# Expert gates: one-hot rows from one broadcast comparison on VectorE, multiplied by the gates on GpSimd

## Chip, cores and metric

One core of one Trainium2 chip runs the whole program in one launch. The metric is device time in microseconds (us); three runs of the kernel before gave 3524.37 us as the median (3522.42 to 3524.39).

## What is computed

Two transformer blocks over 256 tokens of width 2048. The change lies in the last sublayer, a mixture of 16384 single-neuron experts. Each expert is a pair (first key, second key) out of 128 x 128; each of 8 heads chooses 16 of them per token, so 128 slots per token. Cut to what matters:

```python
q = (hb @ w_query).reshape(PEER_BLOCK, PEER_HEADS, 2, D_KEY // 2)
s = jnp.einsum('thpc,hpnc->thpn', q, sub_keys).astype(jnp.float32)
top_s, top_i = lax.top_k(s, PEER_TOPK)
...
best_s, best_j = lax.top_k(cand_s, PEER_TOPK)
idx = jnp.take_along_axis(cand_i, best_j, axis=-1)
g = jax.nn.softmax(best_s, axis=-1)
u_sel = jnp.take(u, idx, axis=0)
a = jax.nn.gelu(jnp.einsum('thkd,td->thk', u_sel, hb), approximate=False)
v_sel = jnp.take(v, idx, axis=0)
return jnp.einsum('thk,thkd->td', (g * a).astype(hb.dtype), v_sel)
```

## The kernel before

**The weight products.** Every large product takes its weights as 128x128 blocks, eight to a DMA of 512 KB. `half` (L285) turns each load into two tiles of four blocks in two parts: ScalarE copies the high part `whi` (through `acp`, L275), VectorE subtracts it from the block for the low part `wlo` (through `vtt`, L260). Four tiles of each part are kept. `linear` makes three TensorE products per block (`mm`, L254): weight high part by activation high part, by activation low part, and weight low part by activation high part.

**The expert stage** (`experts_in`, L1569) does not gather experts. It computes gelu(h . u) of all 16384, in 128 columns of 16 blocks: column c is second key c, with the first keys on the partitions. `expert` (L1605) empties a column: VectorE multiplies the accumulator by the tokens' scale into a tile `et` (two buffers), ScalarE applies the gelu (L272), and for tokens whose gates are known GpSimd multiplies it with the gates that stand in `A` (`gtt`, L257). After the last column, `experts_out` (L1745) multiplies `A` with the second table of weights.

**The gates** (`gates`, L1626) are worked out beside these products, two tokens at a time, 128 pairs of tokens. For a token, slots lie on the partitions. `TI` and `TJ` hold for each slot and token the first and the second key, `TG` the gate in two parts. A tensor_scalar on VectorE compares a row of 0 to 127 (`iota`, in the tile named `ones`) with the slot's first key: `Pt`, a one-hot row per slot (`ts`, L267). Two more tensor_scalars compare with the second key and multiply by one part of the gate: `Qt`, two one-hot rows scaled (L269). TensorE multiplies `Pt` by `Qt` into `pG`: the sum over slots, [first key, part, second key]. `add` (L1634) adds the two parts (ScalarE copies one out, VectorE adds the other: the tile `G`, one buffer), and GpSimd then writes four pieces of `A` for these two tokens: a product (L257) for columns that are done, a copy (L1645) for columns to come.

**The order.** `drive` (L326) goes through the weight blocks and after every sixth takes one step of a stream; here the stream is the choice of keys for tokens 0 to 127 (`choose`), that for tokens 128 to 255, and `gates`. `gates` has two steps per pair: the one-hot rows; then the product `pG` and the `add` of the pair before. With `pace=(1,)` a step's instructions may not issue before the last `wlo` emitted so far. The framework's planner, from its own costs, sets the order on each engine; the engines then work in that order and wait by semaphores. The loads of weights carry high priority.

The lines that make the rows:

```python
Pt = sp.tile([128, n, 128], F32R, name="Pt", tag="Pt", bufs=2)
Qt = [sp.tile([128, 2, 128], F32R, name="Qt", tag="Qt", bufs=3) for _ in range(n)]
for t in range(n):
    o = slice(t0 + t, t0 + t + 1)
    self.ts(Pt[:, t], iota, self.TI[:, o], None, OP.is_equal)
    a, b = divmod(t0 + t, 16)
    for i in range(2):
        self.ts(Qt[t][:, i], iota, self.TJ[:, o], tg[i][:, a, b:b + 1], OP.is_equal, OP.mult)
```

Of the kernel before, what the change touches and what calls it, by code (L numbers as in the profile page):

```python
# [8 lines left out]
F32 = mybir.dt.float32  # L9
# [19 lines left out]
# ---------------------------------------------------------------- host layout  # L29


def _const_arrays():
    """Constants that follow from the shapes alone: name -> [128, width]."""
# [73 lines left out]
# w_in columns in the order in which they are worked on, as (first column, count) pieces of 128-column tiles  # L107
# [25 lines left out]
def _blocks(w, order="cols", group=None):  # L133
    """[K, N] -> [n, 128, 8, 128]: 128x128 blocks in the order in which they are used, eight to a load."""
    k, n = w.shape
    b = w.reshape(k // 128, 128, n // 128, 128)
    if group is None:
        b = b.transpose(2, 0, 1, 3).reshape(-1, 128, 128)
    else:
        kt = k // 128  # L140
        b = b.reshape(kt // group, group, 128, n // 128, 128).transpose(0, 3, 1, 2, 4).reshape(-1, 128, 128)
    return np.ascontiguousarray(b.reshape(-1, 8, 128, 128).transpose(0, 2, 1, 3))


def _pcol(v):
    """[128 * n] -> [128, n]"""
    return np.ascontiguousarray(np.asarray(v).reshape(-1, 128).T)
# [30 lines left out]
def _tT(x):  # L178
    """[T, 2048] -> [128, 16, T]"""
    x = np.asarray(x)  # L180
    return np.ascontiguousarray(x.reshape(x.shape[0], KT, 128).transpose(2, 1, 0))
# [40 lines left out]
# ---------------------------------------------------------------- kernel  # L222
# [4 lines left out]
# weight blocks between the stages of the streams beside them: block 1 (three streams), block 2, the experts  # L227
EVERY1, EVERY2, EVERY3 = (6, 6, 7), 8, 6
QB = 4  # weight blocks in a tile of parts
RAW, PARTS = 4, 4  # tiles of weights as they come; of their high and of their low parts  # L230
# [13 lines left out]
class Kernel:  # L244
# [7 lines left out]
    # ---- small helpers  # L252
# [31 lines left out]
    # ---- weight stream: 128x128 blocks as two float32r parts whose sum is the block  # L284
# [20 lines left out]
    def linear(self, w, h0, ncol, nkt, xh, xl, n, evac, t0=0, c0=0, more=()):  # L305
        """out[col] = sum_kt w[kt, col].T @ (xh + xl)[kt]; n tokens from t0; evac(col, psum)."""
        blk = h0 * 8
        cur = None
        for c in range(c0, c0 + ncol):
            p = self.ps("plin") if c in more else self.plin.tile([128, 512], F32, name="plin", tag="plin")  # L310
            nn = n(c) if callable(n) else n
            tt = t0(c) if callable(t0) else t0
            xs = slice(tt, tt + nn)
            for kt in range(nkt):
                if blk % 8 == 0 or cur is None:
                    cur = self.ahead.pop(0) if self.ahead else self.half(w[blk // 8])
                b = blk % 8
                hi, lo = (self.block(x, b) for x in cur)
                self.mm(p[:, :nn], hi, xh[:, kt, xs], kt == 0, False)
                self.mm(p[:, :nn], hi, xl[:, kt, xs], False, False)  # L320
                self.mm(p[:, :nn], lo, xh[:, kt, xs], False, kt == nkt - 1)
                blk += 1
                yield
            evac(c, p[:, :nn])

    def drive(self, dense, streams, every, pace=(), flush=True):  # L326
        """Emits the weight products with the stages of the other streams between them."""
# [26 lines left out]
    def split(self, hi, lo, src, scale=None):  # L354
        """src (* scale) as hi + lo, float32r each."""
        if scale is None:
            self.acp(hi, src)
            self.vtt(lo, src, hi.bitcast(F32), OP.subtract)
        else:
            self.acp(hi, src, scale=scale)  # L360
            self.stt(lo, src, scale, hi.bitcast(F32), OP.mult, OP.subtract)

    def rsqrt(self, y, x, scale=None, eps=None, floor=None):
        """y = 1 / sqrt(x * scale + eps) for a few columns (x in PSUM or SBUF): Newton from an exponent guess."""
# [15 lines left out]
    def colsum(self, srcs, n):  # L380
        """sum over partitions (and over the tiles srcs) by token -> psum [tokens, block]."""
# [7 lines left out]
    def bcast(self, dst, r, n, o=0):  # L389
        """r [token, block] -> dst [128, n]: the token's value in every partition."""  # L390
# [9 lines left out]
    # ---- whole program  # L400
# [23 lines left out]
    # ---- block 1: RWKV group and sparse attention group  # L424
    def load_norm(self, src, gain, xh, xl, dst, eps, acc, w, tiles):
        """x^T * gain as two parts, and dst = the tokens' 1 / rms in every partition; the first weights come between."""
# [18 lines left out]
    def squares(self, t, acc, first, pool=False):  # L445
        """acc (+)= the squares of a tile [feature, 4, token], in two parts; the tile is overwritten"""
# [17 lines left out]
    def block1(self, c0):  # L464
# [33 lines left out]
        def loads():  # L498
            """the constants, behind the weights that are wanted sooner"""
# [74 lines left out]
        def hold(what):  # L574
            """the recurrent group's stages up to the one that frees a tile"""
# [38 lines left out]
    def inv_sqrt(self, r, x, t):  # L614
        """r = x ** -0.5: an exponential, and a step of Newton's; t is scratch"""
# [6 lines left out]
    def rwkv_group(self, g, AR, K, V, fr):  # L622
# [14 lines left out]
        # decay: exp of minus the running sum, inside chunks of 64 tokens  # L637
# [9 lines left out]
        # unit keys  # L647
# [4 lines left out]
        # decay: exp of minus the running sum, inside chunks of 64 tokens  # L652
# [6 lines left out]
        # token-major copies: partition (chunk parity, token)  # L659
# [14 lines left out]
        # k' = k (1 + (a - 1) k_a)  # L674
# [10 lines left out]
        # scaled factors: A = -kk W_{t-1}, R = r W_t, B = kk a / W_t, K = k' / W_t  # L685
# [24 lines left out]
        # Gram matrices, transposed: [s, (t of A | t of R)]  # L710
# [19 lines left out]
        # F = T^T, T = (I - N)^-1: 32-row diagonal blocks by doubling the block size, then the block below them  # L730
# [25 lines left out]
        # U = T (A S' + A_k V) = P S' + Q  # L756
# [79 lines left out]
        # from chunk to chunk: S' = W_C (M S + R), M = I + B'^T P, R = B'^T Q + K'^T V  # L836
# [47 lines left out]
        # y^T [v, t]  # L884
# [23 lines left out]
        # group norm per head, gate  # L908
# [24 lines left out]
    # ---- sparse attention group  # L933
# [12 lines left out]
    def tables(self):  # L946
        """cosines and sines of the rotary angles, by feature and token"""
# [45 lines left out]
    def rope(self, dst, rot, d):  # L993
        """dst = rope(dst / rms) in place."""
# [58 lines left out]
    def dsa_topk(self):  # L1053
        """mb = 0 where a key is among the 64 best causal ones of its query, else -1e30."""
# [50 lines left out]
    # ---- the rest of block 1  # L1105
    def norm_tile(self, k, src, gain, xh, xl, acc, pool):
        """one feature tile of the next product's input, and its squares"""
# [56 lines left out]
    def cross(self, cp, cxh, cxl, rc):  # L1164
# [57 lines left out]
        # the first columns' products with the heads that are done, between the stages of the last head  # L1222
# [29 lines left out]
    def mlp(self, up):  # L1252
# [43 lines left out]
        # x1 = h g_f r1; block 2 normalises x1: r12 = r1 * rsqrt(r1^2 mean((h g_f)^2) + eps)  # L1296
# [13 lines left out]
    def meta_tokens(self):  # L1310
        """their part of block 2's normalised input"""
# [19 lines left out]
    # ---- block 2: stick-breaking and forgetting attention  # L1331
    def block2(self):
# [33 lines left out]
        def forget(p):  # L1366
            """B16, X16: rows from which a product of 16 gives the sums of log f between two tokens"""
# [14 lines left out]
        def values(t):  # L1382
            """[feature, token] -> [token, block, feature]"""
# [8 lines left out]
        def stick(hd, q_, k_, v_):  # L1392
# [16 lines left out]
            # sums of softplus over the visible keys from s on  # L1409
# [19 lines left out]
        def fox(hd, q_, k_, v_):  # L1429
            # q and k normalised over the head's features  # L1430
# [59 lines left out]
        def merge(acc, src, gain, o, name):  # L1490
            """heads normalised over 1024 features (and gated), as parts of the next product's input"""
# [60 lines left out]
        # token-major copy of the residual, kept in DRAM until the end  # L1552
# [15 lines left out]
    # ---- experts  # L1568
    def experts_in(self):  # L1569
        """gelu(h . u) of every expert, feature rows of the first key on partitions; meanwhile the choice of experts."""  # L1570
# [7 lines left out]
        self.TI, self.TJ = (sp.tile([128, S], F32, name=n) for n in ("TI", "TJ"))  # L1578
        # the gates' two parts, in the columns of the meta tokens, which are free here
# [25 lines left out]
        def expert(c, p):  # L1605
# [4 lines left out]
            t = sp.tile([128, S], F32, name="et", tag="et", bufs=2)  # L1610
# [15 lines left out]
    def gates(self, slot):  # L1626
        """A[first key, second key, token] *= summed gates of the chosen pairs (kept there where A is still to come)"""
# [21 lines left out]
        tg = [x.bitcast(F32) for x in self.TG]  # L1649
        for t0 in range(0, S, n):  # L1650
            yield
            Pt = sp.tile([128, n, 128], F32R, name="Pt", tag="Pt", bufs=2)
            Qt = [sp.tile([128, 2, 128], F32R, name="Qt", tag="Qt", bufs=3) for _ in range(n)]
            for t in range(n):
                o = slice(t0 + t, t0 + t + 1)
                self.ts(Pt[:, t], iota, self.TI[:, o], None, OP.is_equal)
                a, b = divmod(t0 + t, 16)
                for i in range(2):
                    self.ts(Qt[t][:, i], iota, self.TJ[:, o], tg[i][:, a, b:b + 1], OP.is_equal, OP.mult)
            yield  # L1660
            p = self.ps("pG").rearrange("p (t i j) -> p t i j", t=n, i=2)
            for t in range(n):
                self.mm(p[:, t], Pt[:, t], Qt[t])
# [6 lines left out]
    def choose(self, tb, sc, buf, big):  # L1670
        """The 16 best pairs of keys per head, and their softmax: TI, TJ, TG [slot = (head, rank), token]."""
# [68 lines left out]
        for i, t in enumerate((self.TI, self.TJ)):  # L1740
            self.acp(t[:, ts], p[:, 128 * i:128 * i + 128])
# [51 lines left out]
```

## Time and profile before

| what | value |
|---|---|
| median of three runs | 3524.37 us |
| span of the profiled execution | 3527.4 us |
| PE (TensorE matmul) busy | 3471.3 us, 98% |
| DVE (VectorE) busy | 2502.3 us, 71% |
| ACT (ScalarE) busy | 1814.6 us, 51% |
| POOL (GpSimd) busy | 671.6 us, 19% |
| moved by DMA | 602.39 MB, 171 GB/s |
| expert columns, first to last emptied | 2053.3 to 2823.4 us |
| gates, first to last one-hot row | 2237.7 to 2816.0 us |

The profile is of one further execution. The page gives its span, from the first to the last instruction, and no other time for it; the span is 3.0 us (0.09%) over the median of the timed runs. Matmuls overlap, so "PE 98%" says that TensorE always had one in flight, not that it ran at its peak; how many matmuls start in a stretch says how fast it went. A row's idle time is that of its engine, and what ended it is inferred from semaphores.

### The profile page before, as it was taken

The numbers are of one execution on the slowest core, as the hardware profiler recorded it, in microseconds if no ns is written. First come the engines' busy times: TensorE is split into PE (matmuls) and PEld (weight loads), VectorE is DVE, ScalarE is ACT, GpSimd is POOL, SyncE is SP. The second block draws the span as 40 slices with busy tenths as digits, with TensorE's granted clock in tenths as the row PEclk, the third lists the DMA queues.
The fourth block names the chain that finished last, engine by engine and source line by source line (L and its number), as shares of the span: only waits on it lengthen the run. The fifth ranks groups of instructions, "written<-read, shape, count | busy, mean of one in ns | idle before, by whom it ended". The sixth has DMA issues, their size and how long they took to land.

```text
span 3527.4 us, 74174 instructions
## 1 busy us (share of the span) xinstructions
PE 3471.3 (98%) x28638; PEld 3277.4 (93%) x28638; DVE 2502.3 (71%) x5118; ACT 1814.6 (51%) x3416; POOL 671.6 (19%) x1142
## 2 busy tenths in 40 slices
PE   8999999999999999999999999999999999999999
PEld 7899889899999999999999999999999988888887
DVE  7678767765656568556567589999999955555555
ACT  5444555554545455444445444555555555555554
POOL 2222213310101015200012001344445500000000
PEclk9999999999999999999999999999999999999999
DMA  5334536466666666544446655555565566666665
GB/s 195 112 118 129 163 112 189 134 186 184 186 182 186 184 186 183 154 145 143 121 130 186 200 179 163 166 177 178 176 178 177 176 210 193 195 192 195 193 193 183
DMA packets 165779, 602.39 MB, mean 171 GB/s; under 512 B 18384, under 2 KB 19088, under 8 KB 165040
## 3 DMA queue, kind: packets, MB, share of 16 engines
q1 hardware_dynamic: 165424, 597.65, 56.3%
q8 instruction: 224, 3.67, 0.4%
q14 instruction: 131, 1.07, 0.1%
HBM read 593.38 MB, written 4.19 MB: 169 GB/s over the span
## 4 chain that ended last, share of the span: by engine, by line
PE 94%; DVE 4%; issue 1%; DMA 1%; POOL 0%; ACT 0%; DVEq 0%; SPq 0%; ACTq 0%; POOLq 0%
PE plin L254 66%; PE o L254 20%; DVE wlo L260 2%; PE pG L254 1%; PE po L254 1%; PE pfz L254 1%; PE pw L254 0%; PE pz L254 0%; PE pbc L254 0%; PE pix L254 0%; PE pcs L254 0%; DVE xl L263 0%; PE pt L750 0%; PE px L750 0%; PE py L254 0%
## 5 line engine op out<-in xcount | busy, mean ns | idle before, releaser
L260 DVE TENSOR_TENSOR wlo<-raw,whi 128x512 fp32r<-128x512 f32 x2208 | 1610.7, 733 | 809.3 <-ACT whi L275 761.2
L275 ACT ACTIVATE whi<-raw 128x512 fp32r<-128x512 f32 x2208 | 1389.2, 631 | 1333.2 <-PE plin L254 936.6
L254 PE MATMUL plin<-ph,wlo 128*128 128x256 f32 (+1 forms) x4560 | 1290.6, 284 | 11.0 <-DVE wlo L260 11.0
L254 PE MATMUL plin<-ph,whi 128*128 128x256 f32 (+1 forms) x4560 | 1287.9, 283 | 1.6 <-DVE ut L260 0.7
L254 PE MATMUL plin<-pl,whi 128*128 128x256 f32 (+1 forms) x4560 | 1288.7, 283 | 0.0
L254 PEld LDWEIGHTS plin<-ph,wlo 128*128 128x128 f32 x4560 | 863.4, 190 | 15.8 <-DVE wlo L260 13.5
L254 PEld LDWEIGHTS plin<-ph,whi 128*128 128x128 f32 x4560 | 864.1, 190 | 3.0 <-issue 1.6
L254 PEld LDWEIGHTS plin<-pl,whi 128*128 128x128 f32 x4560 | 861.2, 189 | 1.6 <-issue 1.1
L254 PE MATMUL o<-wlo,wh 128*128 128x512 f32 x1024 | 399.1, 390 | 0.0
L254 PE MATMUL o<-whi,wl 128*128 128x512 f32 x1024 | 397.2, 389 | 0.0
L254 PE MATMUL plin<-xh,whi 128*128 128x256 f32 x1136 | 330.6, 292 | 8.7 <-ACT whi L275 8.2
L254 PE MATMUL plin<-xh,wlo 128*128 128x256 f32 x1136 | 329.8, 291 | 3.4 <-DVE wlo L260 3.2
L254 PE MATMUL plin<-xl,whi 128*128 128x256 f32 x1136 | 329.5, 290 | 1.7 <-DVE xl L263 1.7
L254 PE MATMUL o<-whi,wh 128*128 128x512 f32 x1024 | 316.6, 390 | 1.9 <-ACT wh L275 1.9
L254 PE MATMUL plin<-uh,wlo 128*128 128x256 f32 x1024 | 289.7, 283 | 0.0
L254 PE MATMUL plin<-ul,whi 128*128 128x256 f32 x1024 | 289.7, 283 | 0.0
L254 PE MATMUL plin<-uh,whi 128*128 128x256 f32 x1024 | 289.6, 283 | 0.0
L254 PEld LDWEIGHTS plin<-xh,whi 128*128 128x128 f32 x1136 | 222.0, 196 | 13.6 <-ACT whi L275 9.4
L254 PEld LDWEIGHTS o<-whi,wh 128*128 128x128 f32 x1024 | 192.8, 188 | 42.2 <-ACT wh L275 2.1
L254 PEld LDWEIGHTS plin<-xh,wlo 128*128 128x128 f32 x1136 | 221.7, 195 | 10.2 <-DVE wlo L260 5.2
L254 PEld LDWEIGHTS o<-wlo,wh 128*128 128x128 f32 x1024 | 192.8, 188 | 40.2
L254 PEld LDWEIGHTS o<-whi,wl 128*128 128x128 f32 x1024 | 192.1, 188 | 39.9
(571 smaller groups left out, 3866.1 us busy)
## 6 DMA issues: line engine op xcount, KB each, us to landing
raw<-in_pu_dram SPq DMA_DIRECT2D x256, 512.0 KB, 3.7
raw<-in_pv_dram SPq DMA_DIRECT2D x256, 512.0 KB, 4.3
raw<-in_w_in_dram SPq DMA_DIRECT2D x208, 512.0 KB, 3.6
raw<-in_w_up_dram SPq DMA_DIRECT2D x128, 512.0 KB, 4.3
raw<-in_w_down_dram SPq DMA_DIRECT2D x128, 512.0 KB, 4.2
raw<-in_w_mix_dram SPq DMA_DIRECT2D x32, 512.0 KB, 3.7
raw<-in_w_out_dram SPq DMA_DIRECT2D x32, 512.0 KB, 3.7
raw<-in_w_pq_dram SPq DMA_DIRECT2D x32, 512.0 KB, 3.7
```

The source lines that it names most:

```text
L254: self.nc.tensor.matmul(out, l, r, start=start, stop=stop)
L260: return self.nc.vector.tensor_tensor(out, a, b, op=op)
L275: return self.nc.scalar.activation(out, a, AF.Copy, **kw)
```

## The change

For a pair of tokens, the one-hot rows of both tokens and of both keys are made by one tensor_tensor comparison on VectorE, whose two operands are repeated: `iota` over tokens and keys, and the key indices (now interleaved in one tile `TIJ`) over the 128 positions. GpSimd then multiplies the second key's rows of both tokens by the high part of the gates and, in another instruction, by the low part. The scaled rows `Q` have one buffer, the one-hot rows `E` two; `et` has one buffer where it had two. Texts of comments are dropped too. The core of the diff:

```diff
@@ experts_in
-        self.TI, self.TJ = (sp.tile([128, S], F32, name=n) for n in ("TI", "TJ"))
+        self.TIJ = sp.tile([128, S, 2], F32, name="TIJ")
...
-            t = sp.tile([128, S], F32, name="et", tag="et", bufs=2)
+            t = sp.tile([128, S], F32, name="et", tag="et", bufs=1)
@@ gates
+        sh = [128, n, 2, 128]
         for t0 in range(0, S, n):
             yield
-            Pt = sp.tile([128, n, 128], F32R, name="Pt", tag="Pt", bufs=2)
-            Qt = [sp.tile([128, 2, 128], F32R, name="Qt", tag="Qt", bufs=3) for _ in range(n)]
-            for t in range(n):
-                o = slice(t0 + t, t0 + t + 1)
-                self.ts(Pt[:, t], iota, self.TI[:, o], None, OP.is_equal)
-                a, b = divmod(t0 + t, 16)
-                for i in range(2):
-                    self.ts(Qt[t][:, i], iota, self.TJ[:, o], tg[i][:, a, b:b + 1], OP.is_equal, OP.mult)
+
+            E = sp.tile(sh, F32R, name="E", tag="E", bufs=2)
+            self.vtt(E, iota[:, None, None, :].to_broadcast(sh), self.TIJ[:, t0:t0 + n, :, None].to_broadcast(sh),
+                     OP.is_equal)
+            Q = sp.tile(sh, F32R, name="Q", tag="Q", bufs=1)
+            a, b = divmod(t0, 16)
+            for i in range(2):
+                self.gtt(Q[:, :, i], E[:, :, 1].bitcast(F32), tg[i][:, a, b:b + n, None].to_broadcast([128, n, 128]),
+                         OP.mult)
             yield
             p = self.ps("pG").rearrange("p (t i j) -> p t i j", t=n, i=2)
             for t in range(n):
-                self.mm(p[:, t], Pt[:, t], Qt[t])
+                self.mm(p[:, t], E[:, t, 0], Q[:, t])
@@ choose
-        for i, t in enumerate((self.TI, self.TJ)):
-            self.acp(t[:, ts], p[:, 128 * i:128 * i + 128])
+        for i in range(2):
+            self.acp(self.TIJ[:, ts, i], p[:, 128 * i:128 * i + 128])
```

## Rows read from the trace of the kernel before

**Rows 1.** The page: busy time of each engine, and the 40 slices.
```profile
PE 3471.3 (98%) x28638; PEld 3277.4 (93%) x28638; DVE 2502.3 (71%) x5118; ACT 1814.6 (51%) x3416; POOL 671.6 (19%) x1142
...
PE   8999999999999999999999999999999999999999
...
DVE  7678767765656568556567589999999955555555
...
POOL 2222213310101015200012001344445500000000
```

**Rows 2.** The page: the chain that ended last, by engine.
```profile
PE 94%; DVE 4%; issue 1%; DMA 1%; POOL 0%; ACT 0%; DVEq 0%; SPq 0%; ACTq 0%; POOLq 0%
```

**Rows 3.** Windows of 100 us: length, then PE, PEld, DVE, ACT, POOL; clock; DMA.
```profile
2200.00:2300.00 100.00, 93.95 (x757) 92.56 (x756) 96.22 (x222) 50.69 (x102) 33.73 (x61) 0.97 0.54 165
2300.00:2400.00 100.00, 100.00 (x851) 100.00 (x850) 92.25 (x241) 58.59 (x125) 43.56 (x135) 1.00 0.58 178
...
2500.00:2600.00 100.00, 100.00 (x851) 100.00 (x850) 95.42 (x242) 58.20 (x123) 49.00 (x127) 1.00 0.61 179
...
2700.00:2800.00 100.00, 100.00 (x850) 100.00 (x850) 100.00 (x240) 55.71 (x121) 56.18 (x130) 1.00 0.60 176
```

**Rows 4.** Windows of 20 us around the start and the end of the gates.
```profile
2240.00:2260.00 20.00, 16.24 (x117) 15.46 (x118) 20.00 (x34) 8.77 (x19) 6.75 (x6) 0.91 0.36 112
...
2800.00:2820.00 20.00, 20.00 (x172) 20.00 (x171) 18.65 (x42) 10.07 (x25) 12.15 (x25) 1.00 0.58 177
```

**Rows 5.** Waits of PE from 2050 to 2900 us: total, times, longest.
```profile
PE plin L254 <- DVE wlo L260: 8.7, 9, 2.4
PE pG L254 <- DVE Qt L269: 2.9, 2, 2.6
PE o L254 <- ACT wh L275: 1.9, 1, 1.9
```

**Rows 6.** DVE groups by shape, 2050 to 2826 us: count, busy us, mean ns, idle.
```profile
L260 DVE TENSOR_TENSOR wlo<-raw,whi 128x512 fp32r<-128x512 f32 x511 | 377.2, 744 | 22.8 <-ACT whi L275 19.3
L269 DVE TENSOR_SCALAR Qt<-ones,TJ,pl 128x128 fp32r<-128x128 f32 x256 | 97.8, 382 | 0.0
L269 DVE TENSOR_SCALAR Qt<-ones,TJ,ph 128x128 fp32r<-128x128 f32 x256 | 97.1, 379 | 0.1
L267 DVE TENSOR_SCALAR Pt<-ones,TI 128x128 fp32r<-128x128 f32 x256 | 91.8, 359 | 0.0
...
L260 DVE TENSOR_TENSOR s<-s,ones 128x2048 f32<-128x2048 f32 x4 | 9.2, 2289 | 0.0
```

**Rows 7.** POOL groups by shape, whole span; the last row from the gates' stretch.
```profile
L257 POOL TENSOR_TENSOR acc<-acc,sqt 128x256 f32<-128x256 f32 x75 | 73.7, 983 | 5.4
...
L257 POOL TENSOR_TENSOR us<-us,ut 128x256 f32<-128x256 f32 x64 | 52.2, 816 | 588.4 <-ACT us L272 588.4
...
L257 POOL TENSOR_TENSOR s<-s 128x2048 f32<-128x2048 f32 x6 | 28.8, 4796 | 274.5 <-DVE s L1685 181.4 <-DVE s L260 93.1
...
L257 POOL TENSOR_TENSOR AR<-AR,W 128x512 f32<-128x512 f32 x4 | 13.7, 3420 | 19.7 <-DVE rk L263 19.7
...
L257 POOL TENSOR_TENSOR A<-et,A 128x256 f32<-128x256 f32 x1 | 0.7, 734 | 1.2 <-ACT et L272 1.2
```

**Rows 8.** Timelines of DVE and of POOL: start, us, instruction.
```profile
2244.08 4.61 DVE L267 TENSOR_SCALAR Pt<-ones,TI 128x128 fp32r<-128x128 f32 x1
...
2243.04 5.56 POOL L257 TENSOR_TENSOR s<-s 128x2048 f32<-128x2048 f32 x1 [13.00 <-DVE s L260]
```

**Rows 9.** Tile `G`, whole span: what its engine waited for; who waited for it.
```profile
  POOL A L1645: 24.1, 31
...
  POOL A L257: 180.1, 103
```

**Rows 10.** Timelines of DVE and of POOL: the life of one tile `et`.
```profile
2697.95 0.42 DVE L260 TENSOR_TENSOR et<-plin,rf 128x256 f32<-128x256 f32 x1
...
2699.05 0.62 POOL L257 TENSOR_TENSOR A<-et,A 128x200 f32<-128x200 f32 x1 [2.24 <-DVE wlo L260]
```

## Prediction

> **What bounds the kernel now.** First the page's busy times and slices [rows 1]: TensorE is busy 98% of the span and VectorE is at nine tenths or more in eight slices, 25 to 32, most of them the stretch in which the gates are made. A reader could conclude that VectorE is the bound there. The chain of waits says otherwise: 94% of the time that set the end lies on TensorE, 4% on VectorE, nothing on GpSimd [rows 2]. The windows decide it [rows 3]: from 2300 to 2400 us VectorE is busy 92% and TensorE starts 851 matmuls; from 2700 to 2800 us VectorE is busy 100% and TensorE starts 850, at full clock in both. A VectorE that fills up has cost TensorE nothing; its loaded share is work done ahead. So in this stretch TensorE works at its own pitch, 100 / 851 = 0.1175 us. A pair of tokens takes two steps of six weight blocks, so 36 weight products and two gate products: 38 x 0.1175 = 4.465 us, 128 times. This is the budget of every other engine per pair, and time can be won only where TensorE starts fewer matmuls than this.
>
> There are two such places. From 2240 to 2260 us only 117 matmuls start where 172 are usual [rows 4]: 55 x 0.1163 = 6.4 us lost. TensorE waits 2.9 us for `Qt` there [rows 5], and after such a stop its granted clock falls (0.91 in this window), which makes the loss larger than the wait. The other is the passage into the second table of weights, 1.9 us [rows 5]. Together 8.3 us is the most that the gates can give back; the other waits on `wlo` lie in the choice of keys, mostly before the first one-hot row.
>
> **Part 1, VectorE.** Per pair six tensor_scalars go: 2 x (0.359 + 0.379 + 0.382) = 2.24 us [rows 6]. One comparison 128x512 comes. The nearest row is `wlo`, the same shape, two SBUF inputs and a float32r output: 0.744 us. Repeated operands cost nothing extra: the choice of keys has a repeated comparison 128x2048 of 2.289 us, a quarter of which is 0.57 us [rows 6]. VectorE wins about 1.5 us a pair, 192 us in all. On the path this counts zero, since TensorE was not waiting for it.
>
> **Part 2, GpSimd.** Now it works 43.56 us per 100 us early, 49.00 in the middle and 56.18 late [rows 3]. With 22.4 pairs per 100 us that is 1.94, 2.19 and 2.51 us a pair, and 12.15 / 20 x 4.465 = 2.71 us in the last 20 us [rows 4]. Two products of 128x256 are added. The trace has no product with a repeated gate and a float32r output on GpSimd. The nearest rows, 128x256 with two SBUF inputs, give 0.734, 0.816 and 0.983 us [rows 7]. The outer bounds are an eighth of the 128x2048 rows, 0.60 us, and half of the slowest 128x512 row, 1.71 us. I take 0.82, since that row stands, 64 times, beside the same stream of weight splits. Then GpSimd needs 1.94 + 1.63 = 3.57 us a pair early (80% of 4.465), 3.82 in the middle (86%), 4.14 late (93%) and 4.34 in the last 20 us (97%). It fits, barely. The price at which it stops fitting is (4.465 - 2.51) / 2 = 0.98 us late, 1.14 in the middle and 1.26 early. I count zero here, hidden behind TensorE's own 4.465 us, with nearly nothing to spare at the end.
>
> [...] A long GpSimd product, 2243.04 to 2248.60 us, and a `Pt` that began at 2244.08 us end within 0.1 us of each other; this `Pt`, usually near 0.28 us, took 4.61 us [rows 8]. So a tensor_scalar with one tensor input was held up until GpSimd had done. By this row the six removed instructions competed with GpSimd as `wlo` does: nine competing instructions a pair become four, VectorE keeps some 1.5 us to absorb the new waits, and 0.82 us is a fair price. [...]
>
> **Part 3, the new waits.** `pG` now waits for GpSimd, in whose queue the products stand among the pieces of `A`; these wait for `G` 103 times, 180.1 us [rows 9], and what stands behind waits with them. With one buffer the products of the next pair wait until `pG` has read the last; this leaves most of a pair's 4.465 us for 1.63 us of products. `G` has one buffer too, and ScalarE's copy into it waited for GpSimd 31 times, 24.1 us [rows 9]; behind that copy stand the `whi` copies, and behind these `wlo` and TensorE. Four tiles of parts (16 blocks, 5.6 us of TensorE) cover such waits today and still do if GpSimd lags by less than a pair. `et` with one buffer: a tile lives from 2697.95 to 2699.67 us, 1.7 us [rows 10], of the 6 us between columns; GpSimd would have to lag by another 4 us before VectorE waited. Zero for each, on that condition. The stop at 2246 us I leave as it is: it comes from the same long GpSimd product, and the new products queue behind it just as `Pt` waited for it. The interleaved `TIJ` is four short copies, nothing. At the end the last pieces of `A` can stand behind a pair's two products: 1.6 us, counted as 2. No DMA is added or moved past another.
>
> **Sum.** 0 + 0 + 0 + 2 = +2 us. On the profiled span 3527.4 becomes 3529.4; on the median, 3.0 us lower, 3524.4 becomes 3526 us. A measurement of this kernel tells 0.2%, 7 us, from no change, so the forecast is no measurable change.
>
> **The rivals.**
> *GpSimd becomes the bound (slower).* Place: its queue in the late pairs; price: over 0.98 us a product, queue waits included. At 1.2 us the pair needs 4.91 late and 4.59 in the middle, 0.45 and 0.13 us over; over 43 pairs each that is 25 us: 3549 us. At 1.3 us the three thirds are over by 0.65, 0.33 and 0.08 us: 45 us, 3569 us. For it: 0.983 is a row of this kernel, 75 times, and an in-order queue with waits cannot be filled to 97% for long. Against it: two thirds of the stretch have 14% or more to spare at 0.82.
>
> *The products are much dearer than any plain row*, for the float32r output that no GpSimd row shows. At 1.71 us the thirds are over by 0.90, 1.15 and 1.47 us, 150 us: 3674 us. Against it: on VectorE the float32r output of `wlo` costs no multiple of plain f32 (0.744 us for 512 elements against the 0.57 above).
>
> *VectorE's freed time removes TensorE's stops (faster).* All 8.3 us: 3516 us. For it: `pG` did wait for `Qt`. Against it: the long GpSimd product stays and now also holds the one-hot products.
>
> **How the numbers follow.** Forecast (same) 0.48; GpSimd the bound 0.36; dearer products 0.06; stops removed 0.10. So faster 0.10, same 0.48, slower 0.42. The range goes from the full gain, 3516, to the 1.3 us price, 3570; it leaves out the dear products and the worst of the second case. The forecast's own range is 3518 to 3531.
>
> **What would show it.** Right: 850 or so matmuls per 100 us from 2300 to 2800 us, VectorE near 70 to 80% busy, GpSimd 80 to 97%, products at 0.75 to 0.95 us. Wrong: fewer matmuls late, a wait of `pG` on the POOL product in TensorE's list of waits, GpSimd at 100%, or a longer passage into the second table. A faster kernel would show 172 matmuls from 2240 to 2260 us.

## The result, and the profile after

The changed kernel takes 3557.8 us (median of four runs, 3557.0 to 3560.0) against 3524.4 us before: a ratio of 1.0096 [1.0081, 1.011], 33 us slower. That lies inside the range, but the likeliest case, no measurable change, did not come. The case of GpSimd as the bound came nearest, with a cause that it did not have.

The page of the kernel after: busy times, and the slices of VectorE and GpSimd.

```profile
PE 3482.9 (98%) x28638; PEld 3276.7 (92%) x28638; DVE 2422.5 (68%) x4478; ACT 1781.0 (50%) x3416; POOL 957.1 (27%) x1398
...
DVE  7678767765656568556567599877777755555555
...
POOL 2222222310101015200012011788999910000000
```

Against [rows 1] VectorE falls from nine tenths to seven in the gates' stretch, GpSimd rises from four and five tenths to eight and nine. The windows of the kernel after (columns as in [rows 3]):

```profile
2220.00:2240.00 20.00, 15.49 (x114) 14.88 (x113) 18.79 (x18) 9.85 (x16) 9.27 (x4) 0.91 0.34 106
2240.00:2260.00 20.00, 18.36 (x142) 18.37 (x143) 19.19 (x27) 8.47 (x20) 14.34 (x21) 0.91 0.53 161
...
2300.00:2400.00 100.00, 98.62 (x820) 97.20 (x819) 76.49 (x124) 48.61 (x118) 88.76 (x168) 1.00 0.58 170
2500.00:2600.00 100.00, 96.97 (x781) 93.23 (x781) 74.39 (x118) 47.55 (x114) 90.99 (x161) 1.00 0.56 164
2700.00:2800.00 100.00, 95.28 (x785) 93.08 (x784) 76.86 (x119) 46.46 (x111) 98.38 (x159) 1.00 0.56 164
```

The chain that ended last, on the same page, reads now:

```profile
PE 20%; POOL 0%; issue 0%; DVE 0%; ACT 0%; DVEq 0%
```

It was followed back over a fifth of the span only, through the second table, so unlike [rows 2] it says nothing about the gates; the windows have to. Where [rows 3] have 850 matmuls in 100 us, there are now 820 early, 781 in the middle and 785 late, at a granted clock of 1.00 as before: TensorE is not slowed by its clock, it starts fewer. The whole stretch in one window, before and then after:

```profile
2300.00:2800.00 500.00, 500.00 (x4243) 500.00 (x4242) 479.32 (x1200) 287.86 (x613) 245.22 (x643) 1.00 0.59 177
```

```profile
2300.00:2800.00 500.00, 485.66 (x3976) 473.59 (x3975) 381.46 (x601) 239.35 (x573) 463.82 (x806) 1.00 0.56 166
```

4243 - 3976 = 267 matmuls at 0.1175 us are 31 us: nearly the whole loss lies in these 500 us. (Its busy time falls by 14.3 us only, since matmuls overlap, with records of 0.28 us each at one start every 0.1175 us, so that a short gap between two starts does not show as idle time.) The waits of TensorE after, 2050 to 2950 us (beside [rows 5]), and then the waits of all engines from 2300 to 2840 us:

```profile
PE pG L254 <- POOL Q L257: 17.6, 41, 0.9
PE plin L254 <- DVE wlo L260: 12.1, 8, 3.3
PE o L254 <- ACT wh L275: 1.3, 1, 1.3
```

```profile
ACT G L275 <- POOL A L1645: 106.8, 44, 3.2
...
ACT G L275 <- POOL A L257: 71.6, 56, 1.6
DVE wlo L260 <- ACT whi L275: 71.0, 84, 1.4
```

The kernel before, all engines, 2300 to 2820 us:

```profile
POOL A L257 <- DVE G L260: 158.9, 90, 3.1
...
ACT G L275 <- POOL A L1645: 22.0, 27, 2.6
...
DVE wlo L260 <- ACT whi L275: 17.1, 61, 0.6
...
ACT G L275 <- POOL A L257: 3.9, 6, 1.2
```

The order has turned round. Before, GpSimd waited for `G`. After, ScalarE waits for GpSimd to give `G` back: 106.8 + 71.6 us in place of 22.0 and, over the same stretch, 3.9. Behind that copy stand the `whi` copies, for which VectorE's `wlo` now waits 71.0 us in place of 17.1; and `pG` itself waits for the product `Q`. Two roads lead from GpSimd's queue to TensorE. GpSimd's lines from 2300 to 2800 us, before and then after (count, busy us, mean ns, idle before it):

```profile
L257 POOL TENSOR_TENSOR A<-A,G 128x64 f32<-128x64 f32 (+29 forms) x340 | 151.5, 467 | 191.4 <-DVE G L260 152.1 <-ACT A L272 39.0
L1645 POOL COPY A<-G 128x64 f32<-128x64 f32 (+29 forms) x220 | 63.9, 318 | 0.0
L257 POOL TENSOR_TENSOR A<-et,A 128x24 f32<-128x24 f32 (+41 forms) x83 | 40.4, 486 | 63.2 <-DVE wlo L260 62.1 <-ACT et L272 1.1
```

```profile
L257 POOL TENSOR_TENSOR A<-A,G 128x64 f32<-128x64 f32 (+11 forms) x313 | 213.4, 702 | 27.9 <-DVE G L260 27.3
L1645 POOL COPY A<-G 128x64 f32<-128x64 f32 (+20 forms) x207 | 90.1, 464 | 0.0
L257 POOL TENSOR_TENSOR Q<-E,pl 128x256 fp32r<-128x256 f32 x104 | 74.2, 714 | 0.0
L257 POOL TENSOR_TENSOR Q<-E,ph 128x256 fp32r<-128x256 f32 x104 | 67.2, 646 | 0.0
```

The two products are cheaper than the 0.82 us of the forecast. What grew is work that the diff does not touch: the pieces of `A` from 0.467 to 0.702 us, the copies from 0.318 to 0.464. The timelines of the kernel after show one such piece, VectorE first, then GpSimd (start, us, instruction):

```profile
2761.68 0.42 DVE L260 TENSOR_TENSOR G<-G,pG 128x256 f32<-128x256 f32 x1 [1.11 <-ACT G L275]
...
2763.18 0.90 DVE L260 TENSOR_TENSOR wlo<-raw,whi 128x512 fp32r<-128x512 f32 x1
2764.01 0.88 DVE L260 TENSOR_TENSOR E<-ones,TIJ 128x512 fp32r<-128x512 f32 x1
2764.82 0.69 DVE L260 TENSOR_TENSOR wlo<-raw,whi 128x512 fp32r<-128x512 f32 x1
```

```profile
2761.03 0.20 POOL L1645 COPY A<-G 128x30 f32<-128x30 f32 x1
...
2764.29 0.68 POOL L1645 COPY A<-G 128x28 f32<-128x28 f32 x1
```

A copy of 30 columns took 0.20 us while VectorE was idle (from 2760.57 to 2761.68 us). A copy of 28 columns that began inside the comparison took 0.68 us and ended 0.08 us after it (2764.97 and 2764.89). The stall of [rows 8] thus goes the other way too: here a short piece of GpSimd waited until VectorE's long instruction had let go. That this is what lengthens the others is for the experiments to show.

### The profile page after: what moved, and what is told of

Same layout as the page of the kernel before. It is cut to its first block, busy times and chain, and to the rows that moved or that the text cites. A ratio compares the mean times of both kernels' runs of the same rounds, so it can differ in the third digit from the quotient of the medians.

```text
span 3555.1 us, 74059 instructions
## 1 busy us (share of the span) xinstructions
PE 3482.9 (98%) x28638; PEld 3276.7 (92%) x28638; DVE 2422.5 (68%) x4478; ACT 1781.0 (50%) x3416; POOL 957.1 (27%) x1398
## 5 line engine op out<-in xcount | busy, mean ns | idle before, releaser
L260 DVE TENSOR_TENSOR wlo<-raw,whi 128x512 fp32r<-128x512 f32 x2208 | 1656.2, 754 | 861.2 <-ACT whi L275 811.0
L275 ACT ACTIVATE whi<-raw 128x512 fp32r<-128x512 f32 x2208 | 1369.0, 628 | 1173.8 <-PE plin L254 799.4
L254 PE MATMUL plin<-ph,wlo 128*128 128x256 f32 (+1 forms) x4560 | 1290.7, 284 | 14.3 <-DVE wlo L260 14.3
L257 POOL TENSOR_TENSOR A<-A,G 128x64 f32<-128x64 f32 (+21 forms) x381 | 256.8, 694 | 30.7 <-DVE G L260 29.3
```

The costliest lines, as they stand in the source:

```text
L254: self.nc.tensor.matmul(out, l, r, start=start, stop=stop)
L257: self.nc.gpsimd.tensor_tensor(out, a, b, op=op)
L260: return self.nc.vector.tensor_tensor(out, a, b, op=op)
L275: return self.nc.scalar.activation(out, a, AF.Copy, **kw)
```

## The experiments

A demand is, as in the prediction, the busy time of GpSimd in a window divided by pairs; here the window 2300 to 2800 us, and the pairs are its matmuls divided by 38. Before it is 245.22 / (4243 / 38) = 2.20 us, after 463.82 / (3976 / 38) = 4.43, and TensorE's budget is 4.465. (Where an expectation has a higher figure for the same, it added up durations of instructions, which overlap a little in the trace.)

**Who makes GpSimd's old work longer?** The products go back to VectorE and the comparison stays:

```diff
-                self.gtt(Q[:, :, i], E[:, :, 1].bitcast(F32), ...
+                self.vtt(Q[:, :, i], E[:, :, 1].bitcast(F32), ...
```

> The one broadcast comparison stays; the two products with the gates go from GpSimd to VectorE. Queue theory (GpSimd's queue became the bound): GpSimd falls back to about 2.0 to 2.7 us a pair, TensorE gets its 851 matmuls per 100 us back, and the time is 3520 to 3528 us. Comparison theory (the long comparison on two repeated operands is what hurts, by holding VectorE and GpSimd up): most of the 33 us stay, 3545 us or more. Buffer theory (one tile Q, one tile et): part stays, about 3535 to 3550 us.

Measured: 3538.9 us, 1.0045 [1.0028, 1.0062]. GpSimd's lines of this run, 2300 to 2800 us:

```profile
L257 POOL TENSOR_TENSOR A<-A,G 128x64 f32<-128x64 f32 (+18 forms) x329 | 214.8, 673 | 94.3 <-DVE G L260 87.2 <-ACT A L272 6.5
L1645 POOL COPY A<-G 128x64 f32<-128x64 f32 (+20 forms) x212 | 102.7, 512 | 0.0
```

GpSimd executes exactly the instructions of before, and its demand still rises from 2.20 to 362.82 / (4131 / 38) = 3.34 us. Little changed beside it but what VectorE executes: three long instructions with two inputs in place of six tensor_scalars. So GpSimd's work grows by what VectorE does, without an instruction more on its own list. The run loses some 15 us (3538.9 against 3524.4 in the same set of runs) although GpSimd is far from full. ScalarE waits for `G` nearly as long as in the change (132.8 + 28.0 us from 2300 to 2840 us), and VectorE, which now has the products too, is 94 to 95% busy in every 100 us (it was as busy before and cost nothing [rows 3]). Which of the two makes this loss was not tested, so these 15 us cannot be taken as a share of the 33.

One product on each engine, `(self.gtt, self.vtt)[i](...)`:

> The comparison stays; the high-part product stays on GpSimd, the low-part product goes to VectorE. Queue theory: GpSimd loses about 0.7 us a pair of its 4.4 to 4.9, so it fits into 4.465 us nearly everywhere: 3524 to 3532 us. Buffer theory: Q and et still have one buffer, so most of the loss stays: 3545 to 3555 us.

Measured: 3550.2 us, 1.0075 [1.0058, 1.0092], between the two, with 769 matmuls in the late 100 us. The demand is 420.63 / (4055 / 38) = 3.94 us, and dividing the products brings nothing that the run before had not.

**Is it the comparison's form?** Products on GpSimd, the comparison again as four tensor_scalars:

```diff
-            self.vtt(E, iota..., self.TIJ[...]..., OP.is_equal)
+            for t in range(n):
+                for i in range(2):
+                    self.ts(E[:, t, i], iota, self.TIJ[:, t0 + t, i:i + 1], None, OP.is_equal)
```

> The products stay on GpSimd; the comparison is made by four tensor_scalars of 128x128 in place of one tensor_tensor of 128x512. Queue theory with short holds (GpSimd's pieces wait for the whole of the VectorE instruction in front of them, so four short ones delay them less than one long): pieces of A fall from 0.70 us towards 0.6, and the time comes to 3540 to 3553 us. Plain queue theory (only the two products count): 3555 to 3562 us. Comparison theory: back to 3524 us.

Measured: 3525.5 us (ten runs), 1.0006 [0.9996, 1.0015]: the loss is gone. VectorE's and GpSimd's lines of this run, 2300 to 2800 us:

```profile
L267 DVE TENSOR_SCALAR E<-ones,TIJ 128x128 fp32r<-128x128 f32 x440 | 135.3, 366 | 0.0
```

```profile
L257 POOL TENSOR_TENSOR A<-A,G 128x64 f32<-128x64 f32 x336 | 163.0, 506 | 25.5 <-DVE G L260 24.7 <-ACT A L272 0.5
L257 POOL TENSOR_TENSOR Q<-E,pl 128x256 fp32r<-128x256 f32 x111 | 94.7, 853 | 0.0
L257 POOL TENSOR_TENSOR Q<-E,ph 128x256 fp32r<-128x256 f32 x111 | 90.3, 814 | 35.9 <-PE pG L254 14.7 <-DVE E L267 9.8 <-PE plin L254 3.7
```

VectorE spends more time on the comparison, 135.3 / 110.8 = 1.22 us a pair in place of 0.76, and GpSimd's pieces fall to 0.506 us, its demand to 3.96. The products, though, rise from 0.714 and 0.646 to 0.853 and 0.814 us: which of GpSimd's instructions is held up differs from run to run, and only the demand, their sum, can be compared. So VectorE's busy time is not what GpSimd pays for.

**And without any comparison?** `E` is filled for the first two pairs and then read as it is:

```diff
+        Es = [sp.tile(sh, F32R, name="E", tag="E", bufs=2) for _ in range(2)]
...
-            self.vtt(E, iota..., self.TIJ[...]..., OP.is_equal)
+            E = Es[t0 // n % 2]
+            if t0 < 2 * n:
+                self.vtt(E, iota..., self.TIJ[...]..., OP.is_equal)
```

> As changed, but the comparison is made for the first two pairs only, and the rows of these two are used for all the others: the comparisons of the other 126 pairs are left out; both products stay on GpSimd. If the comparison is the whole cost: 3520 to 3528 us, pieces of A at 0.5 us. If the two products load GpSimd too far by themselves: 3540 us or more, with GpSimd over 95% busy late.

Measured: 3520.5 us, 0.9994 [0.9984, 1.0004]. The late window of this run:

```profile
2700.00:2800.00 100.00, 100.00 (x851) 100.00 (x850) 66.47 (x105) 54.77 (x122) 96.89 (x172) 1.00 0.59 177
```

With both products on GpSimd, and it 97% busy, TensorE keeps its pitch. The demand is 422.51 / (4244 / 38) = 3.78 us: the prediction had 3.82 for the middle of the stretch. Its sum was about right; the comparison adds 4.43 - 3.78 = 0.65 us, and it had been put at nothing. One thing stays open: the pieces of `A` take 0.565 us here, less than the 0.702 of the change but more than the 0.467 of before, although VectorE makes no rows at all. Why they grow when the products join GpSimd's queue was not looked into, and what the six tensor_scalars cost GpSimd before is shown by no run.

**What of the comparison: its instructions, its inputs, its time?** Three more forms: four tensor_tensors of 128x128, one tensor_scalar of 128x512 and two of these. The last two leave out three and two of the four indices.

```diff
+                    self.vtt(E[:, t, i], iota, self.TIJ[...].to_broadcast([128, 128]), OP.is_equal)
```

> As changed, but the comparison is made by four tensor_tensors of 128x128 (two SBUF inputs each) in place of one of 128x512. The four tensor_scalars of the same size gave 3525 us. Length theory (GpSimd waits for the instruction in front of it, so short ones delay it less): pieces of A near 0.51 us as with the tensor_scalars, 3524 to 3533 us. Form theory (an instruction of VectorE with two SBUF inputs keeps GpSimd out, a tensor_scalar does not): pieces of A stay near 0.70 us, 3548 to 3562 us.

```diff
+            self.ts(E, iota[...].to_broadcast(sh), self.TIJ[:, t0, 0:1], None, OP.is_equal)
```

> As changed, but the comparison is one tensor_scalar of 128x512 with the first slot key of the pair for all four rows: three of the four rows of indices are left out, and the work and its size stay as they are. Form theory: pieces of A near 0.5 us and 3522 to 3530 us. Length theory: as in the change, pieces near 0.70 us and 3548 to 3560 us.

```diff
+            for i in range(2):
+                self.ts(E, iota[...].to_broadcast(sh), self.TIJ[:, t0, i:i + 1], None, OP.is_equal)
```

> As the run with one long tensor_scalar, but with two of them over the whole of the comparison's rows (the second overwrites the first, so again one index stands for the four rows and the other indices are left out). One took 0.47 us where the tensor_tensor takes 0.68: by the slopes 0.27 and 0.53 us of streaming. Two stream for as long as the one tensor_tensor. Time theory (GpSimd pays for the time that VectorE streams through the shared interface): GpSimd's time per pair goes from 4.30 to about 4.6 us and the run to 3545 to 3560 us. Form theory (only instructions with two SBUF inputs count): GpSimd's time per pair stays under 4.4 us and the run at 3523 to 3532 us.

The tile `E` in the runs with four tensor_scalars, four tensor_tensors, one long tensor_scalar and in the kernel after (shortest / median / longest, ns):

```profile
L267 DVE TENSOR_SCALAR E<-ones,TIJ x512: 270/316/768, 2230.2 to 2812.4; 128x128 fp32r<-128x128 f32 x171
```

```profile
L260 DVE TENSOR_TENSOR E<-ones,TIJ x512: 276/370/809, 2227.9 to 2821.3; 128x128 fp32r<-128x128 f32 x171
```

```profile
L267 DVE TENSOR_SCALAR E<-ones,TIJ x128: 471/501/840, 2235.0 to 2813.5; 128x512 fp32r<-128x512 f32 x128
```

```profile
L260 DVE TENSOR_TENSOR E<-ones,TIJ x128: 677/733/1101, 2231.1 to 2843.1; 128x512 fp32r<-128x512 f32 x128
```

From the shortest ones, 384 more elements cost a tensor_scalar 471 - 270 = 201 ns and a tensor_tensor 677 - 276 = 401 ns: 0.52 and 1.04 ns an element. In these runs a tensor_scalar needs half the time for an element; the rest of either at 128 elements, 0.20 and 0.14 us, is taken as fixed, since only two sizes were measured. Elements times slope is taken here as the time for which an instruction moves data, an estimate:

| comparison of a pair | moves data, us (worked out) | VectorE busy, us | GpSimd's demand, us | more than with none | matmuls 2700 to 2800 | time, us | ratio |
|---|---|---|---|---|---|---|---|
| none | 0 | 0 | 3.78 | 0 | 851 | 3520.5 | 0.9994 [0.9984, 1.0004] |
| four tensor_scalars 128x128 | 0.27 | 1.22 | 3.96 | 0.18 | 819 | 3525.5 | 1.0006 [0.9996, 1.0015] |
| one tensor_scalar 128x512 | 0.27 | 0.53 | 4.10 | 0.32 | 827 | 3524.1 | 1.0001 [0.9992, 1.0011] |
| four tensor_tensors 128x128 | 0.53 | 1.43 | 4.23 | 0.45 | 790 | 3538.5 | 1.0043 [1.0027, 1.0060] |
| one tensor_tensor 128x512 (the change) | 0.53 | 0.76 | 4.43 | 0.65 | 785 | 3557.8 | 1.0096 [1.0081, 1.0110] |
| two tensor_scalars 128x512 | 0.54 | 1.10 | 4.48 | 0.70 | 780 | 3544.8 | 1.0064 [1.0048, 1.0081] |

Of three things that could set the price, the number of instructions (4, 1, 4, 1, 2 down the table) does not order the demand, VectorE's busy time does not, and the time in which data is moved does: what GpSimd pays lies between two thirds and 1.3 times of what VectorE needs to move the comparison's data. The form is not the cause, since two long tensor_scalars, with one tensor input each, cost as much demand as the one tensor_tensor. Short instructions cost 0.14 to 0.2 us less than long ones of the same sum. So the run with four tensor_tensors came out between its two expectations, and the one with one long tensor_scalar had the time of the form theory with pieces of `A` at 0.624 us, not 0.5. Within the table the time follows in steps: up to a demand of 4.10 there is no loss that the time tells, from 4.23 there is one of 16 to 33 us. Demand is not all that sets the time, though: with one product or both on VectorE 26 and 15 us were lost at 3.94 and 3.34. Between the last two rows demand is the same within 0.05 us and the loss differs by some 12 us; what makes that difference was not found. The order of instructions, laid by a planner from costs, is not the same in the two.

**Which road to TensorE costs more?** Two buffers for `G` (and, to make room, `TIJ` as bfloat16, so this is not one change alone):

```diff
-            g = sp.tile([128, n, 128], F32, name="G", tag="G", bufs=1)
+            g = sp.tile([128, n, 128], F32, name="G", tag="G", bufs=2)
```

> Products and comparison as changed; the tile G gets a second buffer, for which the key indices are kept in bfloat16 to make room (whole numbers up to 127). Buffer theory (ScalarE's copy into the only G waits for GpSimd's pieces and holds the whi copies behind it): ScalarE's waits on POOL (178 us from 2300 to 2840 us) mostly go and the time falls to 3530 to 3545 us. Queue theory: GpSimd stays near 98% busy late, and the time stays at 3550 us or more, with a gain of a few us early, where GpSimd was 89% busy.

Measured: 3540.1 us, 1.0048 [1.0031, 1.0065]. ScalarE's wait for the pieces of `A`, 2050 to 2950 us, and the windows of this run:

```profile
ACT G L275 <- POOL A L257: 4.6, 4, 1.9
```

```profile
2300.00:2400.00 100.00, 100.00 (x851) 100.00 (x849) 80.25 (x129) 58.69 (x123) 89.40 (x173) 1.00 0.60 179
...
2700.00:2800.00 100.00, 93.93 (x775) 91.85 (x774) 83.32 (x118) 53.75 (x113) 100.00 (x158) 1.00 0.53 162
```

Early, TensorE has its 851 matmuls back; late, GpSimd is busy for the whole 100 us and TensorE starts 775. So of the 33 us about 18 came by way of the one `G`, which turned a demand just under the budget into stops, if the bfloat16 indices do nothing by themselves, which was not shown (the comparison takes 0.864 us on average from 2300 to 2800 us, and 0.762 in the change); the other 16 remain where GpSimd is full.

Two buffers' worth of `Q`: `E` with three rows a token, into whose last two the products are written, so that `Q` alternates as `E` does (the comparison writes the first and the third):

```diff
-            E = sp.tile(sh, F32R, name="E", tag="E", bufs=2)
+            E = sp.tile([128, n, 3, 128], F32R, name="E", tag="E", bufs=2)
...
-                self.gtt(Q[:, :, i], E[:, :, 1]...
+                self.gtt(E[:, :, 1 + i], E[:, :, 2]...
```

> As changed, but the scaled rows have two buffers: a tile of three rows per token holds the first key's row and the second key's row, and the products write the high and the low part there, the low one in place, so that no more memory is taken. If the single buffer of Q matters (products wait for the last pG): 3540 to 3552 us. If not: 3553 to 3561 us, with GpSimd as full as in the change.

Measured: 3568.1 us, 1.0130 [1.0113, 1.0147], slower than the change, with waits of ScalarE for `G` as long as after (109.4 and 73.2 us). The one buffer of `Q` is not what costs. Why this version takes some 11 us more was not settled.

**The stop at the start of the gates.** The change left it: from 2220 to 2260 us 114 + 142 = 256 matmuls start after, 136 + 117 = 253 before. It comes from GpSimd's products of 128x2048 in the choice of keys. In the kernel before, the three instructions of that shape (a sum, two products) go to VectorE:

```diff
-        self.gtt(cand, ..., OP.add)
+        self.vtt(cand, ..., OP.add)
...
-            self.gtt(eq, eq, ip[...]..., OP.mult)
+            self.vtt(eq, eq, ip[...]..., OP.mult)
```

> The kernel before, with the three long elementwise instructions of each choice of keys (128x2048, one sum and two products) on VectorE in place of GpSimd. If a long GpSimd product keeps VectorE out for all of its 4 to 5 us, as the Pt of 4.61 us says, then six such stops of VectorE become six instructions of 2.3 us: TensorE's stops from 2100 to 2260 us, 17.6 us in all, shrink by half or more, 3508 to 3518 us. If VectorE is only loaded more by it: 3524 to 3535 us.

Measured: 3508.3 us, 0.9958 [0.9941, 0.9974], faster than both kernels. One such product in the kernel before: the windows, VectorE's timeline and GpSimd's.

```profile
2120.00:2140.00 20.00, 17.57 (x137) 17.36 (x136) 19.48 (x22) 9.18 (x15) 6.47 (x2) 0.91 0.48 154
2220.00:2240.00 20.00, 17.71 (x136) 17.30 (x135) 18.50 (x29) 9.46 (x17) 5.07 (x1) 0.91 0.51 153
```

```profile
2124.14 5.93 DVE L260 TENSOR_TENSOR wlo<-raw,whi 128x512 fp32r<-128x512 f32 x3
```

```profile
2123.37 4.95 POOL L257 TENSOR_TENSOR s<-s 128x2048 f32<-128x2048 f32 x1 [34.81 <-DVE s L260]
```

The same windows with these instructions on VectorE:

```profile
2120.00:2140.00 20.00, 19.90 (x167) 19.46 (x165) 19.84 (x32) 11.85 (x20) 0.00 (x0) 1.00 0.56 163
2220.00:2240.00 20.00, 18.17 (x144) 17.02 (x143) 20.00 (x39) 10.44 (x19) 3.59 (x4) 1.00 0.49 144
2240.00:2260.00 20.00, 19.46 (x162) 19.04 (x162) 20.00 (x56) 11.08 (x26) 7.15 (x19) 1.00 0.60 185
```

While the GpSimd product ran, three `wlo` took 5.93 us where three at the mean of 0.744 us [rows 6] take 2.2; TensorE waited 2.4 us for `wlo`, and its granted clock then fell: 0.50 from 2130 to 2132 us, 0.91 over the window. On VectorE the same instruction takes 2.28 us. The three windows hold 473 matmuls in place of 137 + 136 + 117 = 390: 83 at 0.1163 us are 9.7 of the 14 us (3508.3 against 3522.6).

Both together, the change with four tensor_scalars and these three instructions on VectorE:

> Four tensor_scalars make the comparison, GpSimd the products (3525 us by themselves), and the three long instructions of each choice of keys go to VectorE (3508 us by themselves, in the kernel before). If the two add up: TensorE's stops from 2100 to 2260 us shrink as they did there, the 6 us of stops after 2650 us stay, 3507 to 3514 us. If GpSimd's fuller queue meets VectorE's fuller start: 3515 to 3525 us.

Measured: 3514.9 us, 0.9977 [0.9966, 0.9987]: faster than before. It is some 6 us slower than the last run, by medians from two sets of runs, and the two intervals overlap. Late the 818 matmuls of the four tensor_scalars stand again (819 there). No version here shows that moving the products to GpSimd pays.

## What was right and what was wrong in the prediction, point by point

3557.8 us lies in the range of 3516 to 3570, but outside 3518 to 3531, the range of the forecast itself. The upper end of the wide range is the rival's product at 1.3 us, and the products took 0.68 us on average: that the range holds the time is luck as far as the mechanism goes.

**Bound and budget: right.** TensorE's pitch and 4.465 us a pair hold: in the run without the comparison 851 matmuls start, with GpSimd at 97%.

**Part 1, VectorE: right on the path, too large in size.** VectorE's busy time per pair falls from 479.32 / 111.7 = 4.29 to 381.46 / 104.6 = 3.65 us, 0.65 and not 1.5. The comparison at 0.762 us is the 0.744 of the forecast. But the 2.24 us for six tensor_scalars added up durations that overlap: before, VectorE's groups sum to 565.6 us in these 500 us and it was busy for 479.32, after they sum to 411.7 with 381.46 busy. And `wlo`, 0.711 us on average over these 500 us before, takes more:

```profile
L260 DVE TENSOR_TENSOR wlo<-raw,whi 128x512 fp32r<-128x512 f32 x314 | 256.6, 824 | 70.7 <-ACT whi L275 65.7
L260 DVE TENSOR_TENSOR E<-ones,TIJ 128x512 fp32r<-128x512 f32 x105 | 80.0, 762 | 0.0
```

(VectorE's groups of the kernel after, 2300 to 2800 us.) On TensorE it is worth nothing, as forecast.

**Part 2, the products: the sum right, its terms not.** 0.82 us a product was too high for this kernel. Tile `Q` of the kernel after:

```profile
L257 POOL TENSOR_TENSOR Q<-E,ph x128: 605/612/1149, 2231.9 to 2845.5; 128x256 fp32r<-128x256 f32 x128
L257 POOL TENSOR_TENSOR Q<-E,pl x128: 605/612/1154, 2232.8 to 2846.1; 128x256 fp32r<-128x256 f32 x128
```

The median is 0.612 us, near the lower bound of 0.60, and the mean 0.68 from 2300 to 2800 us; neither the float32r output nor the repeated gate shows as a price. In the run without the comparison two products take 145.0 / 111.7 = 1.30 us a pair in place of 1.63, and the older work about 2.48 in place of 2.19. The two errors cancel, which is luck: 3.82 against 3.78 us.

**GpSimd and VectorE side by side: the step that failed.** "Nine competing instructions a pair become four", so that the older work would stay at 1.94 to 2.51 us. Counting instructions was the error: it put the comparison's price for GpSimd at zero. The runs show 0.65 us a pair, and 3.82 becomes 4.43, with 4.465 to spend. Without the products' own time the older work went from 2.20 us a pair to about 2.48 with the products and no comparison, and to about 3.08 with it. The six removed instructions could compete, as their `Pt` of 4.61 us shows [rows 8], and so could `wlo`, as the three that took 5.93 us beside a GpSimd product show. But a tensor_scalar needed 0.52 ns an element where a tensor_tensor needed 1.04: an estimate for six, if all move at the measured slope, is 6 x 128 x 0.52 ns = 0.40 us, and the comparison has 0.53 us, more and in one piece. These 0.13 us do not account for the rise over before; that part stays open. Why the two engines hold each other up is not shown either: the "shared interface" of an expectation above is the author's assumption, and the runs show a price only, 0.65 us a pair for one tensor_tensor and 0.70 for two tensor_scalars of that size, about the time for which their data moves by the estimate, 0.53 and 0.54 us.

**Part 3, the new waits.** `et` with one buffer: right, no wait of VectorE for GpSimd. `Q` with one buffer: right that the buffer is free, but the product itself came late, 17.6 us in 41 waits. `G` with one buffer: wrong. The condition, that GpSimd lags by less than a pair, failed with the demand, and some 18 us came this way (the run with two `G`). The passage: 2 us forecast, TensorE's wait there is 1.3 us against 1.9 before [rows 5].

**The rivals.** GpSimd as the bound happened in its place. Its price, "over 0.98 us a product, queue waits included", holds if everything that GpSimd gained is laid on two products, (4.43 - 2.20) / 2 = 1.12 us. But at 1.12 us the rival's own sum gives only the late third, (2.51 + 2.23 - 4.465) x 43 = 12 us, or 3536; that 3558 lies between its 3549 and 3569 for 1.2 and 1.3 us is chance. The mechanism was another: not the products' own rows became dear but those beside them, and the loss began early (820 matmuls), where the rival had 1.26 us as the price at which it stops fitting. Its argument that an in-order queue cannot be filled to 97% for long did not hold: without the comparison GpSimd is 97% busy from 2700 to 2800 us and TensorE loses nothing. The dear product and the removed stops did not come: products are cheap, and the stop at 2246 us stayed, as the prediction said, because the long GpSimd product stays.

## What to carry to other kernels

GpSimd had two loads here: its own instructions and what VectorE's comparison added to them, 3.78 and 0.65 us a pair in the change. Before moving work to GpSimd, or joining VectorE's small instructions into one long tensor_tensor, sum the time in which VectorE's instructions move data (elements times the slope between two sizes of the same form), not instructions and not busy time, and add it to GpSimd's demand; this is an estimate, and for the five comparisons of this case it was right to within a third. A demand 5% under the budget was a loss here already, since a single buffer tied the queue to the engine that sets the pace, and with the products on VectorE one 25% under it was, for a reason that is open. A long GpSimd instruction beside a stream that VectorE feeds was better on VectorE here, even a loaded one (14 us).

## What the runs showed of the hardware that was not expected

- A GpSimd copy of 30 columns took 0.20 us alone, one of 28 columns 0.68 us beside a tensor_tensor of 128x512. The hold goes both ways: three `wlo` took 5.93 us beside one GpSimd product of 4.95 us.
- GpSimd makes a 128x256 product with a repeated operand and a float32r output in 0.61 us (median; mean 0.68), less than any of its rows with two full inputs of that size, whose means are 0.73 to 0.98 us [rows 7].
- TensorE gained when VectorE took over work in stretches where it was already 92 to 100% busy: the instruction of 128x2048 took 2.28 us there against 4.8 us on GpSimd [rows 7], which had kept VectorE out for as long.
